# Six of sixteen projection tiles as pairs, with operand sums stored by the attention blocks and the mLSTM packed into the first six tiles

## The chip, the cores and the metric

The kernel runs on one core of one Trainium2 chip. The metric is the device time of one execution in microseconds (us), and lower is better. Engines are called by the names of the profile: PE is the matrix engine (PEld its weight loads), DVE the vector engine, ACT the scalar engine, POOL the general engine and SP the queue that issues most transfers.

## The reference

One inference step of a hybrid decoder layer on 512 prompt tokens and 8 x 4 sample tokens. In the kernel a token's column index runs over T = 544. An input projection feeds an mLSTM branch (4 heads of 512) and a sliding-window attention branch (32 heads of 64, window 128). Each branch is projected with a 2048 x 2048 matrix, gated, added, projected once more and normalised. The part that the change touches:

```python
br_m = hn.reshape(B, T, M_WIDTH) * jax.nn.sigmoid(o_m) * jax.nn.silu(z_m)
br_a = h_a * jax.nn.silu(z_a)
y = (jax.nn.sigmoid(g_m) * jnp.einsum('btc,cd->btd', br_m, w_proj_m)
     + jax.nn.sigmoid(g_a) * jnp.einsum('btc,cd->btd', br_a, w_proj_a))
out = jnp.einsum('btc,cd->btd', y, w_out)
return _layernorm(DN_ALPHA * x + out, ln_w, ln_b).astype(x.dtype)
```

Everything is float32. The kernel keeps that precision on PE by splitting each operand into a high and a low part (`hilo` for activations, `split` for weights: a cast on ACT and a subtraction on DVE) and adding three products: high x high, high x low, low x high.

## The kernel before

Activations lie transposed, channels on partitions and tokens along the row. A projection makes 128 output channels at a time, a column tile `ct`. There are two ways to do it.

**Plain** (`gemm`, `products`): 16 row blocks k of 128, three products each, two column halves of 272 tokens (HT = 272), so 96 matmuls into two PSUM banks. Weights come as two halves of 512 KB into three buffers (`wr`) and are split.

**Pairs** (`paired`, `prepare`, `half_product`, `gather`): two column tiles at once by a seven-product scheme of the Strassen kind over the 2 x 2 blocks (k below and above 8, tokens below and above 272). Each product is 8 row blocks x 3 = 24 matmuls. It needs sums of the operand's blocks, here called s1, n2, n3 and s4, each split into two parts, and sums of weight blocks, made by DVE (L665) and by accumulating transfers on POOL's queue (L663). The first input projection runs as pairs for most of the kernel; w_proj_m and w_out run four plain tiles first, while `operand_sums` builds their sums, and then pairs.

Helper work is written as generators. `spawn` puts one on a list, and `tick` advances each of the list by one step, from inside `products` (after every `every` row blocks) or after each product of `paired`. `drain` ticks until the list is empty. The order on each engine comes from a list scheduler that goes by the order of the program, by `high_priority` and by its own cost model. `issue_after(x)` makes the instructions of the block on x's engine stand behind x.

The stages, in order: the input projection in pairs, with the attention blocks beside it (`attention`, k = 0 to 15, each ending with a product on POOL, L848, and a store of its branch rows to d_bra, L849, on SP), then `sample_attention` and the sample heads of the mLSTM; w_proj_a with 16 plain tiles (from 1757 us), beside which `mlstm` runs the four prompt heads; w_proj_m; w_out and the layer norm. Nothing of w_proj_a runs as pairs, since the sums of its operand do not exist.

One head of the mLSTM: `values` (four transposes, split into vh, vl), `keys` (transposes, weighting L1427, split, 24 matmuls L1438 for the new state), `cells` (scores L1470, weighting L1473, split, matmuls L1483, `layernorm_rows`, transposes and row products L1494, store to d_brm). vh, vl, dm, ph and pl have one buffer each. The projection takes two of the four banks of pool psA per tile (`bank`), the helpers take banks of psB (`sm`, four). When the mLSTM has ended, `branch(d_brm, ...)` loads and splits the mLSTM branch for w_proj_m (L1377, then L245 and L246).

## Time and profile before

| | |
|---|---|
| time, median of 3 runs | 2464.07 us (2462.01 to 2466.16) |
| profiled execution, its own time | 2464.16 us |
| its span, first to last instruction | 2462.4 us |
| PE busy | 2433.8 us, 99% |
| DVE / ACT / POOL busy | 1884.0 / 1215.4 / 509.9 us |
| mean granted PE clock | 0.997 |
| transfers | 464.72 MB, mean 189 GB/s |

The profile is one execution recorded by the hardware. Busy time is the share in which an engine had an instruction at work; matmuls overlap, so a busy PE says that it was never idle, not that it ran at its peak. In a group of instructions, "xN" is their number, then come the total busy time, the mean length of one in ns, and the idle time of the engine ahead of them with what ended it. In a window's row the columns are the stretch, its length, the busy time and count of PE, PEld, DVE, ACT and POOL, the granted clock, the DMA share and GB/s. A line such as "SPq L187 <- DVE wl L201: 54.1, 10, 10.1" says who waited for whom: in total, how often, and the longest.

### The profile page before, as it was taken

How to read it: one execution, taken by the hardware profiler on the slowest of the kernel's cores; microseconds unless marked ns; L12 is line 12 of the kernel's file. 1: busy time of each engine (PE TensorE's matmuls, PEld its weight loads, DVE VectorE, ACT ScalarE, POOL GpSimd, SP SyncE). 2: the span in 40 equal slices, each digit the busy share in tenths (PEclk: the TensorE clock that was granted, in tenths of full speed). 3: DMA queues.
4: the chain of work that ended last, by engine and by line, in shares of the span. 5: the costliest groups of instructions: out<-in, count | busy, mean ns of one | idle time of the engine just before them, and what ended most of it. 6: DMA issues, size and time to landing. Idle time of an engine off the chain costs nothing.

```text
span 2462.4 us, 48812 instructions
## 1 busy us (share of the span) xinstructions
PE 2433.8 (99%) x19446; PEld 2378.9 (97%) x19446; DVE 1884.0 (77%) x2813; ACT 1215.4 (49%) x1994; POOL 509.9 (21%) x478
## 2 busy tenths in 40 slices
PE   8999999999999999999999999999999999999997
PEld 8999999999999999999999999999999999999996
DVE  7768888888888887787887888878855654767657
ACT  5456676676676564433433444544633333344431
POOL 3114334334333331211121122210000000110111
PEclk9999999999999999999999999999999999999998
DMA  6866666666666644578587687576755546888876
GB/s 177 201 173 158 163 161 144 162 161 150 160 154 160 155 124 138 143 217 247 179 242 244 163 241 229 176 251 217 246 171 173 187 147 210 226 218 253 220 221 188
DMA packets 557436, 464.72 MB, mean 189 GB/s; under 512 B 45592, under 2 KB 454344, under 8 KB 556952
## 3 DMA queue, kind: packets, MB, share of 16 engines
q1 hardware_dynamic: 540312, 402.09, 55.1%
q0 software_dynamic: 15696, 57.15, 12.1%
q8 instruction: 153, 2.51, 0.4%
q10 hardware_dynamic: 1200, 2.36, 0.3%
q14 instruction: 75, 0.61, 0.1%
HBM read 319.06 MB, written 96.31 MB: 169 GB/s over the span
## 4 chain that ended last, share of the span: by engine, by line
PE 94%; DMA 3%; DVE 2%; issue 1%; ACT 1%; SPq 0%; DVEq 0%; POOL 0%; ACTq 0%; POOLq 0%
PE bank L685 46%; PE bank L687 23%; PE bank L210 11%; PE sm L1438 2%; PE sm L210 1%; PE bank L1250 1%; PE sm L1470 1%; PE sm L795 1%; PE sm L1483 1%; PE sm L841 1%; DMA tx<-d_y 1%; DMA ty<-d_y 1%; DMA raw<-in_w_in 1%; PE sm L1800 1%; PE sm L821 1%
## 5 line engine op out<-in xcount | busy, mean ns | idle before, releaser
L200 ACT CAST wh<-raw 128x1024 fp32r<-128x1024 f32 x632 | 662.7, 1049 | 836.2 <-PE bank L685 686.6
L201 DVE TENSOR_TENSOR wl<-raw,wh 128x1024 fp32r<-128x1024 f32 x632 | 792.2, 1255 | 194.6 <-ACT wh L200 175.3
L685 PE MATMUL bank<-xk,wh 128*128 128x272 f32 x2336 | 322.7, 289 | 0.0
L665 DVE TENSOR_TENSOR raw<-raw,raw 128x1024 f32<-128x1024 f32 x238 | 304.1, 1279 | 12.6 <-DMA raw<-in_w_in 8.3
L685 PEld LDWEIGHTS bank<-xk,wh 128*128 128x128 f32 x2336 | 303.0, 188 | 2.8 <-issue 2.4
L704 POOL TENSOR_TENSOR ev<-p,ev 128x272 f32<-128x272 f32 x82 | 117.9, 1438 | 458.3 <-ACT ev L703 401.2
L685 PE MATMUL bank<-n2h,wh 128*128 128x272 f32 x656 | 169.8, 291 | 0.2 <-ACT wh L200 0.2
L687 PE MATMUL bank<-xk,wl 128*128 128x272 f32 x1168 | 169.7, 288 | 0.0
L685 PE MATMUL bank<-n3h,wh 128*128 128x272 f32 x656 | 169.6, 291 | 0.0
L685 PE MATMUL bank<-s1h,wh 128*128 128x272 f32 x656 | 169.1, 291 | 0.0
L685 PE MATMUL bank<-n2l,wh 128*128 128x272 f32 x656 | 167.7, 288 | 0.0
L685 PE MATMUL bank<-n3l,wh 128*128 128x272 f32 x656 | 167.6, 288 | 0.0
L685 PE MATMUL bank<-s1l,wh 128*128 128x272 f32 x656 | 167.3, 287 | 0.0
L685 PE MATMUL bank<-s4h,wh 128*128 128x272 f32 x656 | 167.2, 289 | 0.0
L685 PE MATMUL bank<-s4l,wh 128*128 128x272 f32 x656 | 167.0, 287 | 0.0
L687 PEld LDWEIGHTS bank<-xk,wl 128*128 128x128 f32 x1168 | 155.6, 188 | 0.1
L685 PE MATMUL bank<-a11h,wh 128*128 128x272 f32 x584 | 150.6, 290 | 0.0
L685 PE MATMUL bank<-a11l,wh 128*128 128x272 f32 x584 | 149.4, 288 | 0.0
L210 PE MATMUL bank<-bh,wl 128*128 128x272 f32 x704 | 147.5, 290 | 0.7 <-DVE wl L201 0.7
L210 PE MATMUL bank<-bh,wh 128*128 128x272 f32 x704 | 148.1, 289 | 0.0
L210 PE MATMUL bank<-bl,wh 128*128 128x272 f32 x704 | 148.0, 289 | 0.0
L663 POOL DMA_DIRECT2D raw<-raw x90 | 78.1, 868 | 291.8 <-DVE ev L712 202.2
(493 smaller groups left out, 5670.4 us busy)
## 6 DMA issues: line engine op xcount, KB each, us to landing
raw<-in_w_in SPq DMA_DIRECT2D x296, 512.0 KB
raw<-raw POOLq DMA_DIRECT2D x90, 512.0 KB, 4.8
C<-in_state_mlstm_C SPq DMA_DIRECT2D x32, 1024.0 KB
out<-C SPq DMA_DIRECT2D x64, 512.0 KB
raw<-in_w_proj_a SPq DMA_DIRECT2D x32, 512.0 KB
raw<-in_w_proj_m SPq DMA_DIRECT2D x32, 512.0 KB
raw<-in_w_out SPq DMA_DIRECT2D x32, 512.0 KB
d_v<-ev SPq DMA_DIRECT2D x16, 272.0 KB
```

The costliest lines, as they stand in the source:

```text
L200: state["cast"] = A.copy(wh[:, k:k + n], raw[:, k:k + n])
L201: state["split"] = V.tensor_tensor(out=wl[:, k:k + n], in0=raw[:, k:k + n], in1=r32(wh[:, k:k + n]), op=ALU.subtract)
L210: PE.matmul(ps[f][:, :w], a[:, kk], b(k, c, w), start=(k == 0 and n == 0), stop=(k == 15 and n == 2))
L663: G.dma_start(out=w[out][:], in_=w[b][:], accum_op=ALU.add)
L665: V.tensor_tensor(out=w[out][:], in0=w[a][:], in1=w[b][:], op=ALU.add)
L685: PE.matmul(ps, wh[:, k], x(p, k), start=(first and k == 0 and p == 0), stop=False, skip_group_check=True)
L687: state["end"] = PE.matmul(ps, wl[:, k], x(0, k), start=False, stop=(k == 7), skip_group_check=True)
L704: G.tensor_tensor(out=c22, in0=p1, in1=c11, op=ALU.subtract)
L795: PE.matmul(pp[:, c0 + w0:c0 + 256], qs[a][:, j * 128:j * 128 + 128], kx[:, k0:k0 + 256 - w0], start=(n == 0), stop=(n == 1))
L821: PE.transpose(pt[:, b * 128:b * 128 + 128], s_[:, b, 128:256], ident)
L841: PE.matmul(po[:, b * 128:b * 128 + n], VA[:, b], p_[:, 2 * b:2 * b + n // 128], start=(b == 0 and m == 0), stop=(b == 3 and m == 1), skip ...
L1438: PE.matmul(pp[:, 0:258], a[:, b * 128:b * 128 + 128], b_[:, b, f], start=(b == 0 and n == 0), stop=(b == 3 and n == 2))
```

## The change

- PSUM pools are closed and opened again: 4 + 4 banks up to the projection, six for helpers and two for the projection in it (`psum_pools(6)`), 4 + 4 again from the first pair. PSUM tiles of a new pool wait tile by tile for those that they replace.
- Attention blocks k = 8 to 15 load the first 240 columns of both halves of block k - 8's rows into a score buffer, form the four sums with DVE and store them to a new array, d_sa. `sample_attention` does the same for the 32 remaining columns ("rim" and samples), with one more load and four stores, all in pieces of 32 columns.
- w_proj_a: tiles 0 to 5 are plain with more frequent ticks (every row block in the first half, every second in the second). From tile 2 on PE's instructions of a tile stand behind the last mLSTM matmul that was written when the tile before began. Then `drain`; tiles 6 and 7 plain, while `stored_sums` loads and splits the 16 stored sums into the buffers that the mLSTM left; tiles 8 to 13 as three pairs; tiles 14 and 15 plain, with the loads and splits of the mLSTM branch beside them.
- mLSTM: the loads of values, keys and gate rows of a head are issued during the head before; the row output is a task of its own; queries are split beside the keys; two copies (L1442, L1519) go from DVE to ACT.

```diff
@@ -80,6 +80,7 @@
         kw = {"space": space} if space is not None else {}
         if space is None:
             kw["side"] = side or "right"
+        if space is not bass.MemoryType.DRAM:
             kw["reuse_waits"] = "tile"
         return stack.enter_context(tc.tile_pool(name=name, bufs=bufs, **kw))
...
-    psB = pool(es, "psB", 4, PSUM)
-    psA = pool(es, "psA", 4, PSUM)
-
     dr = pool(es, "dr", 1, bass.MemoryType.DRAM)
+
+    esPS = ExitStack()
+    es.callback(esPS.close)
+
+    def psum_pools(n):
+        return pool(esPS, nm("psB"), n, PSUM), pool(esPS, nm("psA"), 8 - n, PSUM)
 
...
+
+    psB, psA = psum_pools(4)
 
     def sm():
         return psB.tile([128, 512], F32, tag="sm", name=nm("sm"))
...
+    d_sa = dr.tile([8, 128, 4, T // 2], F32, name="d_sa")
...
-            products(ps, half, wh, wl, xh, xl, cols, every)
+            products(ps, half, wh, wl, xh, xl, cols, every[half] if isinstance(every, tuple) else every)
...
-    def paired(work, plain=None):
+    def paired(work, plain=None, rest=()):
 
         steps = [(w, n) for w in work for n in range(7)]
         ready = 0
...
+            if at == 4:
+                for _ in rest:
+                    pass
             half_product(w, n)
             with tc.high_priority(offset=AHEAD):
                 gather(w, n)
...
+        if k > 7:
+            sc = scores_tile()
+            nc.sync.dma_start(sc[:, 0:4:2, 0:PC], d_bra[k - 8].rearrange("p (c x) -> p c x", c=2)[:, :, 0:PC])
         for a in range(2):
...
         G.tensor_tensor(out=hT[:], in0=sz[:, 0:SEQ], in1=hT[:], op=ALU.mult)
         nc.sync.dma_start(d_bra[k][:, 0:SEQ], hT[:])
+        if k > 7:
+            spawn(branch_sums(sc[:, :, 0:PC], hT[:, 0:PC], hT[:, HT:SEQ], d_sa[k - 8][:, :, 0:PC]))
+
+    PC = SEQ - HT
+
+    def branch_sums(t_, r12, r22, to):
+        r11, s1, r21, s4 = (t_[:, j] for j in range(4))
+        V.tensor_tensor(out=s1, in0=r22, in1=r21, op=ALU.subtract)
+        V.scalar_tensor_tensor(r21, r11, -1.0, r21, op0=ALU.mult, op1=ALU.subtract)
+        V.tensor_tensor(out=r11, in0=r11, in1=s1, op=ALU.subtract)
+        V.tensor_tensor(out=s4, in0=r12, in1=r11, op=ALU.subtract)
+        if to is None:
+            for j in range(4):
+                nc.sync.dma_start(d_sa[:, :, j, PC:HT].rearrange("k p t -> p k t"), t_[:, j])
+        else:
+            nc.sync.dma_start(to, t_)
+        yield
...
+        left = kb[:].rearrange("p b x -> p (b x)")
+        rim = left[:, 1024:1536].rearrange("p (k t) -> p k t", k=16)
+        with tc.issue_after(state["load"].ins):
+            nc.sync.dma_start(rim, d_bra[:, :, PC:HT].rearrange("k p t -> p k t"))
         PTs = weightsT(0)
         before = iter(())
...
         nc.sync.dma_start(d_bra[:, :, SEQ:T].rearrange("k p t -> p k t"), gas[:])
+        t_ = left[:, 0:1024].rearrange("p (j k t) -> p j k t", j=4, k=8)
+        V.tensor_copy(t_[:, 0], rim[:, 0:8])
+        V.tensor_copy(t_[:, 2], gas[:, 0:8])
+        for _ in branch_sums(t_, rim[:, 8:16], gas[:, 8:16], None):
+            pass
...
-    _, bah, bal, g_ = branch(d_bra, act, lambda k: ev(), ahead)
+    (bah_, bal_), bah, bal, g_ = branch(d_bra, act, lambda k: ev(), ahead)
...
+    esPS.close()
+    psB, psA = psum_pools(6)
...
-                    PE.matmul(pp[:, 0:258], a[:, b * 128:b * 128 + 128], b_[:, b, f],
+                    state["cells"] = PE.matmul(pp[:, 0:258], a[:, b * 128:b * 128 + 128], b_[:, b, f],
...
-        V.tensor_copy(co[:, 256:512], p1[:, 0:256])
+        A.copy(co[:, 256:512], p1[:, 0:256])
...
-    def cells(h, kh, kl, qh, ql):
+    def cells(h, kh, kl, qh, ql, pre):
...
-                        PE.matmul(pp[:, 0:n], x_[c][:, b * 128:b * 128 + 128], y_[c][:, b * 128:SEQ],
+                        state["cells"] = PE.matmul(pp[:, 0:n], x_[c][:, b * 128:b * 128 + 128], y_[c][:, b * 128:SEQ],
...
             yield
+        if h + 1 < MH:
+            pre["v"] = load4(d_v, h + 1)
+        gt = load4(d_g, h)
...
-                            PE.matmul(pp[:, 0:258], x_[:, off:off + 128], y_[:, b, f],
+                            state["cells"] = PE.matmul(pp[:, 0:258], x_[:, off:off + 128], y_[:, b, f],
...
-            yield
-        gt = load4(d_g, h)
+            if js[-1] == 3 and h + 1 < MH:
+                pre["k"] = load4(d_k, h + 1)
+            yield
+        spawn(rows_out(h, hns, gt))
+
+    def rows_out(h, hns, gt):
         for c in range(4):
...
     def mlstm():
+        pre = {"v": load4(d_v, 0)}
+        for _ in range(2):
+            yield
+        pre["k"] = load4(d_k, 0)
+        yield
         for h in range(MH):
-            vts = load4(d_v, h)
+            vts, kts = pre["v"], pre["k"]
             spawn(decays(h))
-            yield
-            kts = load4(d_k, h)
             for c in range(4):
                 yield from values(h, c, vts[c])
             qts = load4(d_q, h)
             kh, kl, qh, ql = [], [], [], []
+
+            def two_parts(src, to):
+                a, b_ = t5(F32R), t5(F32R)
+                hilo(src[:], a[:], b_[:])
+                for tiles, t_ in zip(to, (a, b_)):
+                    tiles.append(t_)
+
             g_ = None
             for c in range(4):
-                a, b_ = t5(F32R), t5(F32R)
-                V.tensor_copy(a[:], kts[c][:])
-                V.tensor_tensor(out=b_[:], in0=kts[c][:], in1=r32(a[:]), op=ALU.subtract)
-                kh.append(a)
-                kl.append(b_)
+                two_parts(kts[c], (kh, kl))
                 n_ = keys(h, c, kts[c])
                 next(n_)
+                if c > 1:
...
+            for c in (2, 3):
+                two_parts(qts[c], (qh, ql))
             for _ in g_:
                 pass
             yield
-            yield from cells(h, kh, kl, qh, ql)
+            yield from cells(h, kh, kl, qh, ql, pre)
...
     wm, wa_, wo = kview("w_proj_m"), kview("w_proj_a"), kview("w_out")
     spawn(mlstm())
-    bmh = None
-    for ct in range(16):
-        sg = c5t()
-        nc.sync.dma_start(sg[:], d_sga[ct])
-        ps = gemm(wa_, ct * 128, bah, bal, every=2)
-        for p_, s_ in halves(ps, sg):
-            V.tensor_tensor(out=s_, in0=p_, in1=s_, op=ALU.mult)
-        nc.sync.dma_start(d_t[ct], sg[:])
-        if bmh is None and (not live or ct == 15):
-            drain()
-            esA.close()
-            es3, esE = ExitStack(), ExitStack()
-            act3 = pool(es3, "act3", 8)
-            bm_, bmh, bml, g_ = branch(d_brm, act3, lambda k: c5t() if k % 2 else ev())
-            spawn(g_)
-            c6 = pool(esE, "c6", 2)
-            esR = ExitStack()
-            wr2, pe_ = pool(esR, "wr2b", 3), pool(esR, "peb", 1)
-            tx = pool(esR, "txb", 2)
-    drain()
     def operand_sums(src, to, p):
 
...
@@ -1598,11 +1632,93 @@
     def operands(tiles, sums):
 
         low = [t[2:] for t in tiles]
-        return [side_by_side(tiles, 0), quarter(sums["s1"]), quarter(sums["n2"]), side_by_side(low, 0),
-                quarter(sums["n3"]), quarter(sums["s4"]), side_by_side(low, HT)]
+        s1, n2, n3, s4 = (x if callable(x) else quarter(x) for x in (sums[n] for n in ("s1", "n2", "n3", "s4")))
+        return [side_by_side(tiles, 0), s1, n2, side_by_side(low, 0), n3, s4, side_by_side(low, HT)]
+
+    def stored_sums(src, to, p):
+        f, e = ([[p.tile([128, 4, 2, HT], F32R, tag="act", name=nm("sum" + n)) for _ in range(2)] for n in "hl"]
+                for _ in range(2))
+        to["n2"], to["s1"], to["n3"], to["s4"] = (
+            (lambda q, k, t=t, j=j: t[q][k // 4][:, k % 4, j]) for t in (e, f) for j in range(2))
+
+        def load(n):
+            t_ = tx.tile([128, T], F32, tag="tx", name=nm("tx")) if n % 7 < 4 else ev()
+            G.dma_start(out=two(t_[:]), in_=src[n % 8][:, 0:2] if n < 8 else src[n % 8][:, 2:4])
+            return t_
+
+        ahead = [load(n) for n in range(7)]
+        for n in range(16):
+            for _ in range(2 if 8 <= n < 12 else 1):
+                yield
+            k, t_ = n % 8, ahead.pop(0)
+            hilo(two(t_[:]), *(t[k // 4][:, k % 4] for t in (e if n < 8 else f)))
+            if n + 7 < 16:
+                ahead.append(load(n + 7))
 
     def c6t():
         return c6.tile([128, T], F32, tag="c6", name=nm("c6"))
+
+    def plain_a(ct, **kw):
+        sg = c5t()
+        with tc.issue_after(state["load"].ins):
+            nc.sync.dma_start(sg[:], d_sga[ct])
+        ps = gemm(wa_, ct * 128, bah, bal, **kw)
+        for p_, s_ in halves(ps, sg):
+            V.tensor_tensor(out=s_, in0=p_, in1=s_, op=ALU.mult)
+        nc.sync.dma_start(d_t[ct], sg[:])
+
+    def pair_a(ct):
+
+        sgs = []
+
+        def early():
+            for c in (ct, ct + 1):
+                sg = c5t()
+                with tc.issue_after(state["load"].ins):
+                    nc.sync.dma_start(sg[:], d_sga[c])
+                sgs.append(sg)
+
+        def end(o1, o2):
+            for c, sg, o in zip((ct, ct + 1), sgs, (o1, o2)):
+                V.tensor_tensor(out=sg[:], in0=o[:], in1=sg[:], op=ALU.mult)
+                nc.sync.dma_start(d_t[c], sg[:])
+        return dict(wv=wa_, x=XA, cA=ct * 128, cB=ct * 128 + 128, scale=1.0, acc=True, end=end, early=early)
+
+    LEAD_A, PAIR_A, TAIL_A = 6, 8, 14
+    marks = []
+    for ct in range(LEAD_A):
+        marks.append(state.get("cells"))
+        with tc.issue_after(marks[ct - 1].ins) if ct > 1 and marks[ct - 1] else ExitStack():
+            plain_a(ct, every=(1, 2))
+    drain()
+    esA.close()
+    es3, esE = ExitStack(), ExitStack()
+    act3 = pool(es3, "act3", 8)
+    c6 = pool(esE, "c6", 2)
+    esR = ExitStack()
+    wr2, pe_ = pool(esR, "wr2b", 3), pool(esR, "peb", 1)
+    esB2 = ExitStack()
+    tx = pool(esB2, "txb", 4)
+    SA = {}
+    sums_ = stored_sums(d_sa, SA, act3)
+    next(sums_)
+    spawn(sums_)
+    for ct in range(LEAD_A, PAIR_A):
+        with tc.issue_after(state["cells"].ins):
+            plain_a(ct, every=2, prio=AHEAD)
+    esPS.close()
+    psB, psA = psum_pools(4)
+    XA = operands((bah_, bal_), SA)
+    paired([pair_a(ct) for ct in range(PAIR_A, TAIL_A, 2)], state["split"], rest=sums_)
+    state["end"] = None
+    drain()
+    esB2.close()
+    tx = pool(esR, "txc", 2)
+    bm_, bmh, bml, g_ = branch(d_brm, act3, lambda k: ev() if k % 5 < 3 else c6t())
+    spawn(g_)
+    for ct in range(TAIL_A, 16):
+        plain_a(ct, every=2, prio=AHEAD)
+    drain()
 
     def merged(ct, plain=False):
 
```

More of the change, by code (lines that the diff above doesn't have):

```diff
@@ L1515, in mlstm @@
             kh, kl, qh, ql = [], [], [], []
+            def two_parts(src, to):
[3 more added lines that the diff above has]
+                    tiles.append(t_)
             g_ = None
             for c in range(4):
-                a, b_ = t5(F32R), t5(F32R)
-                V.tensor_copy(a[:], kts[c][:])
-                V.tensor_tensor(out=b_[:], in0=kts[c][:], in1=r32(a[:]), op=ALU.subtract)
-                kh.append(a)
-                kl.append(b_)
+                two_parts(kts[c], (kh, kl))
                 n_ = keys(h, c, kts[c])
                 next(n_)
+                if c > 1:
+                    two_parts(qts[c - 2], (qh, ql))
                 if g_ is not None:
@@ L1529, in mlstm @@
                 yield
-            for c in range(4):
-                a, b_ = t5(F32R), t5(F32R)
-                hilo(qts[c][:], a[:], b_[:])
-                qh.append(a)
-                ql.append(b_)
+            for c in (2, 3):
+                two_parts(qts[c], (qh, ql))
             for _ in g_:
```

## The prediction

> **What bounds the kernel now.** I read the page first (shares, chain), then the waits of the matmul engine, then busy time by stretch, then groups of instructions inside the projection stage.
>
> ```profile
> span 2462.4 us, 48812 instructions
> ...
> PE 2433.8 (99%) x19446; PEld 2378.9 (97%) x19446; DVE 1884.0 (77%) x2813; ACT 1215.4 (49%) x1994; POOL 509.9 (21%) x478
> ...
> PE 94%; DMA 3%; DVE 2%; issue 1%; ACT 1%; SPq 0%; DVEq 0%; POOL 0%; ACTq 0%; POOLq 0%
> ```
>
> ```profile
> PE bank L210 <- DVE wl L201: 0.7, 1, 0.7
> ```
>
> ```profile
> 520.00:920.00 400.00, 400.00 (x3221) 400.00 (x3220) 337.44 (x486) 260.32 (x475) 146.53 (x110) 1.00 0.64 153
> 850.00:900.00 50.00, 50.00 (x405) 50.00 (x404) 44.00 (x61) 32.03 (x59) 18.17 (x13) 1.00 0.59 146
> 950.00:1000.00 50.00, 50.00 (x369) 46.00 (x368) 38.43 (x63) 25.46 (x51) 7.04 (x4) 1.00 0.34 96
> 1757.00:2013.00 256.00, 255.30 (x2032) 252.93 (x2032) 160.10 (x400) 99.39 (x191) 10.62 (x20) 1.00 0.53 175
> 2125.00:2215.00 90.00, 90.00 (x721) 90.00 (x721) 62.81 (x81) 36.09 (x44) 12.60 (x12) 1.00 0.83 213
> 2200.00:2250.00 50.00, 50.00 (x402) 50.00 (x401) 34.16 (x47) 21.73 (x29) 3.91 (x4) 1.00 0.94 268
> ```
>
> PE carries the chain (94%). From 1752 to 2110 us it waited once, 0.7 us (the second fence). The windows give the stretch, then PE, weight loads, DVE, ACT, POOL (count), granted clock, DMA share, GB/s. The three stages that the edit touches have PE without a gap: the attention blocks (520 to 920; DVE 84%), the mLSTM beside the projection's tiles (1757 to 2013), and pairs (2125 to 2215). So time changes in two ways only: fewer matmuls, or a PE gap that is not there now.
>
> **Part 1, three pairs for six tiles.** A plain tile is 16 row blocks x 3 products x 2 column halves = 96 matmuls of 272 columns, so two tiles are 192. A pair is 7 products x 24 = 168. Three pairs drop 72 matmuls. In the pair window 721 take 90.00 us, 124.8 ns each: 72 x 0.1248 = 9.0 us less.
>
> [...]
>
> Everything else adds no matmul. The question is what of the 9.0 us the rest gives back.
>
> **Part 2, the mLSTM in six tiles.** First the work.
>
> ```profile
> L210 PE MATMUL bank<-bl,wh 128*128 128x272 f32 x340 | 73.0, 291 | 0.0
> L210 PE MATMUL bank<-bh,wh 128*128 128x272 f32 x340 | 72.9, 290 | 0.0
> L210 PE MATMUL bank<-bh,wl 128*128 128x272 f32 x338 | 71.8, 291 | 0.7 <-DVE wl L201 0.7
> ```
>
> ```profile
> L201 DVE TENSOR_TENSOR wl<-raw,wh 128x1024 fp32r<-128x1024 f32 x34 | 41.5, 1219 | 18.8 <-ACT wh L200 18.7
> L1066 DVE BATCH_NORM_STATS2 lnst<-sm 128x6 f32<-128x256 f32 x32 | 13.2, 425 | 0.0
> L1560 DVE TENSOR_TENSOR c<-bank,c 128x272 f32<-128x272 f32 x32 | 12.6, 430 | 12.4 <-PE bank L210 12.2
> ...
> L1494 DVE TENSOR_TENSOR t<-sm,t 128x512 f32<-128x512 f32 x16 | 10.2, 683 | 16.5 <-PE sm L1493 16.5
> ...
> L1442 DVE COPY f<-sm 128x256 f32<-128x256 f32 x16 | 6.8, 422 | 24.1 <-PE sm L1438 24.1
> L1519 DVE CAST t<-t 128x512 fp32r<-128x512 f32 x16 | 6.7, 420 | 1.5 <-DMA t<-d_k 1.5
> ...
> L1068 DVE SCALAR_TENSOR_TENSOR lns<-lns 128x1 f32<-128x1 f32 x16 | 3.5, 219 | 0.5
> ```
>
> Between 1757 and 2013 the projection has 340 + 340 + 338 = 1018 matmuls, 127 us at 124.8 ns (10.6 tiles); the other 129 us are the mLSTM's. Six tiles are 576 matmuls, 71.9 us, so the packed stage is 129 + 72 = 201 us of PE. DVE there has 160.1 now. It loses 4.6 tiles: 9.2 splits x 1.22 = 11.2 and 9.2 evacuations x 0.43 = 4.0. It also loses the copies of L1442 and L1519 that go to ACT, 6.8 + 6.7. That leaves 131 us, 65% of 201. ACT has 99.4 now; with some 16 us added for them it is at 57% even if it lost nothing. Neither engine is the bound by its sum. The head's program takes 15 steps (four values, four keys, one more, three scores, three cells), so 3 + 60 + 4 for the last rows, some 69 with the ends. Six tiles give 6 x (8 + 4) = 72 steps, so it fits.
>
> Order is the danger: a head change, where PE now lives on projection matmuls.
>
> ```profile
> 1883.65 4.00 PE bank L210 x32
> 1888.75 4.50 PE bank L210 x36
> 1895.18 2.88 PE bank L210 x23
> 1899.75 4.98 PE bank L210 x40
> 1906.90 2.68 PE sm L1438 x22
> ```
>
> ```profile
> 1893.96 0.69 DVE L1451 TENSOR_TENSOR f<-sm,cc 128x512 f32<-128x512 f32 x1 [1.55 <-PE sm L1449]
> ...
> 1907.65 2.07 DVE L246 TENSOR_TENSOR t<-t,t 128x512 fp32r<-128x512 f32 x3
> ```
>
> These are pieces of the chain and of DVE's timeline. From the end of one head's cells to the next head's first key product (1906.90) PE does 16.4 us of projection in the four pieces, while DVE runs almost gapless from 1893.96 to 1907.65. After the edit six steps lie there, on average 6 x 1.0 = 6.0 us of projection, and some 42 transposes at 0.124 (400.00 / 3221 in the first window above), 5.2 us: 11.2 us of cover. DVE must do one row normalisation (two statistics of 0.43, eight small operations of at most 0.22, about 2.3), four value splits and four row products at 0.68, the decay's sum (0.69), three operations of 0.68 on the first key, a weight split (1.22) and two evacuations (0.79): 12.5 us. Short by 1.3, with about 2 us of hand-overs 3.3, for each of three changes: at worst 9.9 us. Against it: matmuls of the same tile may be taken early (6 us on average are left of a tile), the row products are now a task behind the next head's first step, and value and key loads are issued during the cells before. The mark on the cells two tiles back only stops the projection from running out too soon. I take a seventh, +1.4 us, nearer to zero because today's waits are zero at nearly the same DVE share (160.1 of 256, 63%); bounds 0 and +9.9.
>
> **Part 3, two banks instead of four for the projection.** A tile must now be evacuated before the next begins.
>
> ```profile
> 2065.72 0.79 DVE L1560 TENSOR_TENSOR c<-bank,c 128x272 f32<-128x272 f32 x2 [3.79 <-PE bank L210]
> 2066.68 1.23 DVE L201 TENSOR_TENSOR wl<-raw,wh 128x1024 fp32r<-128x1024 f32 x1 [0.17 <-ACT wh L200]
> ```
>
> I read the first from the timeline (its pair takes 0.79, one 0.43). Bare, PE waits about 0.43 plus a hand-over of 0.1; behind a weight split, 1.2 more. There are seven such boundaries, tile 0/1 to 6/7. Five lie inside the mLSTM, whose own matmuls fill them; 5/6 and 6/7 are bare, 0.55 each. I take +1.1 us; bounds 0.5 and 7 x 2.0 = 14 us.
>
> [...]
>
> **Part 4, sums in the attention blocks.** Blocks 8 to 15 add one load, four DVE operations and one store each; the sample rows get copies, sums, one load and four stores.
>
> ```profile
> L1587 DVE TENSOR_TENSOR tx<-tx 128x272 f32<-128x272 f32 x2 | 0.9, 430 | 0.0
> ```
>
> ```profile
> SPq L187 <- DMA raw<-raw: 112.3, 22, 11.2
> SPq L849 <- POOL hT L848: 74.5, 9, 10.8
> ```
>
> Four sums of 240 columns cost at most 4 x 0.43 = 1.7 us, eight blocks 13.8 us on DVE, which goes from 84 to 88% there. The window from 850, with 44.00 of 50, already keeps PE at 50.00, and splits are prepared three products (9 us) ahead: zero. SP gets the new store behind the branch store (L849), which already holds that queue for up to 10.8 us; weight loads (L187) stand behind it. The sums add about 2 us to such a hold. The load waits for a score buffer, released some steps before. The cover is the six buffered weight halves; if it goes, 8 x 2 = 16 us is the far bound. I take 0. The sample columns move in pieces of 128 B, but DMA is 0.34 busy from 950 to 1000: 0, at most +2.
>
> **Part 5, the tail's two hand-overs.** The stored sums (16 loads of 272 KB on POOL's queue, 16 splits of 0.72 on DVE) must be ready between 27 and 36 us after tile 6 begins. The mLSTM branch's 16 loads and splits, formerly spread from 1836 on, now fit between the last pair and the end of the first tile of the next product, some 36 us.
>
> ```profile
> L1377 SPq DMA_DIRECT2D ev<-d_brm x8: 319/320/891, 1836.1 to 2024.4; - x8
> ```
>
> ```profile
> L246 DVE TENSOR_TENSOR bl<-c,bh x8: 716/724/726, 2026.9 to 2056.2; 128x544 fp32r<-128x544 f32 x8
> ```
>
> Each is 16 x 0.72 = 11.6 us of DVE in 36. Bytes: 4.4 MB, about 3 MB of weights and 1 MB of other traffic in 36 us, 233 GB/s; 2200 to 2250 carried 268 GB/s with PE at 50.00. I take 0; bounds 0 and +4, one late transfer each.
>
> **Sum.** -9.0 + 1.4 + 1.1 = -6.5 us. The profiled execution took 2464.16 us (span 2462.4 and 1.8 around it), 0.1 above the median of 2464.07: 2457.6 us, 0.26% less. About 0.2%, 4.9 us, can be told from no change, so the stalls may reach 4.1 us before the gain is lost to view.
>
> **Rivals.**
>
> (a) Starved head changes: the cover of part 2 fails and 5 to 9.9 us come back. For: DVE's gapless stretch above. Against: DVE's 65% and the loose tile. With 7.5 + 1.1: 2463.7, within 0.2%.
>
> (b) Two banks bubble, the slower end. At each of the seven boundaries the evacuation stands behind a split or an mLSTM operation on DVE and PE has nothing else: 2.0 us each, 14 us. With part 2's 1.4, -9.0 + 14.0 + 1.4 = +6.4: 2470.5. It decides for slower than before from 7.6 / 7 = 1.1 us a boundary, and visibly from 1.8. Against: 129 us of mLSTM matmuls stand beside 72 us of projection.
>
> (c) SP's queue in the attention blocks: the added holds starve weights for 1.5 us in each of the eight blocks: +12, so -6.5 + 12 = +5.5, 2469.6. Against: PE waits nowhere there though holds reach 10.8 us.
>
> (d) The work of parts 4 and 5 costs nothing and the stalls do not appear: 2455.1.
>
> **Numbers.** Forecast 0.42, (d) 0.12, (a) 0.22, (b) 0.14, (c) 0.10. Faster by over 0.2%: (d), and four fifths of the forecast and a little of (a), 0.48. Within 0.2%: the rest of the forecast and most of (a), 0.28. Slower: (b), (c): 0.24. The faster case's own range is 2454 to 2460. For 8 in 10 the range runs from 2454 (below (d)) to 2470: it takes in (a) and (c) and leaves out about half of (b) and what lies past the bounds.
>
> **What would show it.** PE with 72 fewer matmuls; the stage from the first plain tile to the first pair about 225 us (129 + 8 x 12); PE waits inside it below 3 us, on evacuations at 5/6 and 6/7; PE at 50.00 of 50 in 520 to 920; the projection's last six tiles as pairs at 21 us each. I am wrong if PE's waits on DVE or ACT in that stage sum to over 5 us, if L187's waits on SP reach PE, or if the next product's first tile waits for its operand.

## The result

The changed kernel takes 2472.66 us (median of 7 runs, 2470.57 to 2474.05) against 2464.07 for the kernel before (7 runs, 2461.53 to 2466.16): a ratio of 1.0035, 95% interval 1.0023 to 1.0047, 8.6 us slower. The forecast was 2457.6, the range 2454 to 2470. The sign was wrong, and the time lies past the upper end. The profiled execution took 2474.05 us (span 2472.3), the longest of the seven.

The page of the changed kernel, span, busy times and shares of the chain:

```profile
span 2472.3 us, 48919 instructions
...
PE 2430.4 (98%) x19374; PEld 2372.8 (96%) x19374; DVE 1911.0 (77%) x2856; ACT 1245.6 (50%) x2060; POOL 524.2 (21%) x503
...
PE 88%; DMA 5%; DVE 3%; issue 2%; ACT 1%; SPq 1%; POOL 0%; DVEq 0%; POOLq 0%; ACTq 0%
```

The 72 matmuls are gone (19446 to 19374), yet PE's busy time fell by only 3.4 us while the span grew by 9.9. PE's share of the chain fell from 94 to 88%, and DMA's rose from 3 to 5. New waits ate more than the saved matmuls. The waits of PE over the whole execution of the changed kernel (in total, times, longest):

```profile
PE bank L692 <- ACT wh L207: 5.9, 4, 1.9
...
PE bank L692 <- DVE ev L717: 2.1, 1, 2.1
PE bank L217 <- DVE wl L208: 2.1, 2, 1.4
PE sm L1459 <- DMA t<-d_v: 1.7, 1, 1.7
PE sm L805 <- DVE mn L807: 1.5, 1, 1.5
PE bank L217 <- DVE c L1667: 0.9, 2, 0.5
```

Only the last stands in the prediction's sum. The windows of the changed kernel that answer to those shown before:

```profile
520.00:920.00 400.00, 395.45 (x3174) 394.36 (x3173) 336.05 (x510) 255.43 (x471) 138.56 (x107) 1.00 0.67 163
850.00:900.00 50.00, 50.00 (x405) 50.00 (x404) 41.92 (x65) 31.96 (x59) 17.44 (x14) 1.00 0.62 155
950.00:1000.00 50.00, 49.37 (x449) 46.00 (x448) 38.39 (x62) 25.95 (x52) 6.79 (x5) 1.00 0.38 102
1768.00:2024.00 256.00, 252.38 (x1999) 249.05 (x1999) 169.00 (x395) 123.88 (x245) 21.97 (x35) 1.00 0.62 197
2125.00:2215.00 90.00, 90.00 (x722) 90.00 (x721) 61.94 (x83) 36.15 (x45) 12.50 (x12) 1.00 0.84 214
2200.00:2250.00 50.00, 50.00 (x402) 50.00 (x401) 31.14 (x42) 18.62 (x23) 6.11 (x6) 1.00 0.87 243
```

The attention blocks had 400.00 of 400 and now have 395.45. An average DVE share (336.05 of 400, as low as before) does not show why. First starts of the same work in the two traces tell how the delay grows:

| first start, us | before | after | difference |
|---|---|---|---|
| last attention block's store to d_bra | 911.7 | 918.2 | +6.5 |
| sample attention's gate load | 914.4 | 928.2 | +13.8 |
| attention branch's loads for w_proj_a | 1739.2 | 1750.3 | +11.1 |
| first plain tile of w_proj_a | 1757.1 | 1768.2 | +11.1 |
| first store of y (w_proj_m) | 2094.6 | 2105.7 | +11.1 |
| first product of w_out | 2254.9 | 2265.1 | +10.2 |

So there are two findings. Some 11 us are lost before the projection starts, in the stages that hold only the new sums. And in the stage where 72 matmuls were saved, almost nothing is gained. Of the signs that the prediction named, PE at 50.00 of 50 in 520 to 920 failed, and PE's waits between the first plain tile and the first pair came to 3.7 us instead of less than 3.

**Where the blocks lose: 700 to 750 us.** The next three fences are the SP queue by time: of before, of the changed kernel, and of the run e5 below, in which one load was moved. L769, L779 fetch the key rows of the next head group, L187 and L194 weights, L847 the rows for the sums.

```profile
706.62 1.09 SPq L769 DMA_DIRECT2D s<-d_ka  x2
...
710.62 4.33 SPq L187 DMA_DIRECT2D raw<-in_w_in  x2
```

```profile
706.81 0.54 SPq L847 DMA_DIRECT2D s<-d_bra  x1
710.82 4.39 SPq L194 DMA_DIRECT2D raw<-in_w_in  x2
...
716.01 2.44 SPq L779 DMA_DIRECT2D s<-d_ka  x2
```

```profile
706.08 1.12 SPq L779 DMA_DIRECT2D s<-d_ka  x2
...
710.10 4.37 SPq L194 DMA_DIRECT2D raw<-in_w_in  x2
```

In the changed kernel the sums' load takes the free score buffer at 706.81. The key load gets the next one, which DVE's last read of it (L841) sets free at 715.20:

```profile
714.66 0.54 DVE L841 TENSOR_TENSOR P<-s,P 128x384 fp32r<-128x384 f32 x1
```

A weight load that holds SP for 4.39 us stands ahead of it as well, and ends at the same moment. So it starts at 716.01 instead of 706.62; the buffer alone accounts for 8.6 of these 9.4 us. ACT and DVE pay. ACT by time (L252 casts the keys, L207 weights), and two of DVE's waits in 690 to 760 us, both of the changed kernel:

```profile
723.38 0.62 ACT L252 CAST k<-s 128x512 fp32r<-128x512 f32 x1 [7.16 <-DMA s<-d_ka]
723.91 1.04 ACT L207 CAST wh<-raw 128x1024 fp32r<-128x1024 f32 x1
```

```profile
DVE k L253 <- ACT k L252: 5.0, 1, 5.0
DVE s L807 <- DMA d_sa<-s: 3.8, 1, 3.8
```

ACT's cast of the keys waits 7.2 us for the load (1.0 in the same window of before). The weight cast behind it starts the moment it is done, with no wait of its own: it had only been standing in line, and so had the next pieces of weights that PE needs. DVE stands behind that cast for 5.0 us, and 3.8 us more for the sums' own store, which must leave its score buffer before scores can be written there. The windows of before and of the changed kernel at that place:

```profile
700.00:750.00 50.00, 50.00 (x405) 50.00 (x404) 42.65 (x61) 33.64 (x62) 17.21 (x14) 1.00 0.70 166
```

```profile
700.00:750.00 50.00, 45.45 (x357) 44.36 (x356) 37.43 (x60) 29.24 (x55) 15.12 (x12) 1.00 0.67 159
```

PE lost 4.55 us, and DVE and ACT were both less busy, not more: they waited.

**Where the tail loses: 2048 to 2064 us.** ACT by time in the changed kernel (L252 casts the mLSTM branch, L207 weights), then the chain of waits there:

```profile
2047.44 1.05 ACT L207 CAST wh<-raw 128x1024 fp32r<-128x1024 f32 x1 [0.35 <-PE bank L692]
2054.09 0.65 ACT L252 CAST bh<-ev 128x544 fp32r<-128x544 f32 x1 [5.59 <-DMA ev<-d_brm]
...
2055.18 1.04 ACT L207 CAST wh<-raw 128x1024 fp32r<-128x1024 f32 x1
```

```profile
2048.63 6.01 DMA c<-d_brm
...
2055.18 1.05 ACT wh L207
...
2056.28 2.74 PE bank L692 x16
2059.02 1.81 PE bank L694 x8
```

It is the same pattern: a cast for a product that starts only after two more plain tiles (24 us) waits 5.59 us for its transfer, and the last pair's weight cast stands behind it. PE waits 1.8 us.

### The profile page after: what moved, and what is told of

It reads as the page before. It is cut to its first block, busy times and chain, and to the rows that moved or that the text cites. A ratio compares the mean times of both kernels' runs of the same rounds, so it can differ in the third digit from the quotient of the medians.

```text
span 2472.3 us, 48919 instructions
## 1 busy us (share of the span) xinstructions
PE 2430.4 (98%) x19374; PEld 2372.8 (96%) x19374; DVE 1911.0 (77%) x2856; ACT 1245.6 (50%) x2060; POOL 524.2 (21%) x503
## 4 chain that ended last, share of the span: by engine, by line
PE 88%; DMA 5%; DVE 3%; issue 2%; ACT 1%; SPq 1%; POOL 0%; DVEq 0%; POOLq 0%; ACTq 0%
PE bank L692 44%; PE bank L694 22%; PE bank L217 8%; PE sm L1480 2%; PE sm L217 1%; PE sm L1512 1%; PE bank L1289 1%; PE sm L1528 1%; PE sm L805 1%; PE sm L854 1%; DVE wl L208 1%; PE sm L1916 1%; PE sm L831 1%; PE sm L1294 1%; DMA ty<-d_y 1%
## 5 line engine op out<-in xcount | busy, mean ns | idle before, releaser
L207 ACT CAST wh<-raw 128x1024 fp32r<-128x1024 f32 x641 | 671.8, 1048 | 833.7 <-PE bank L692 701.8
L672 DVE TENSOR_TENSOR raw<-raw,raw 128x1024 f32<-128x1024 f32 x244 | 311.9, 1279 | 17.5 <-DMA raw<-in_w_proj_a 4.7
L670 POOL DMA_DIRECT2D raw<-raw x96 | 83.1, 866 | 327.5 <-DVE ev L719 203.6
L692 PEld LDWEIGHTS bank<-n2h,wh 128*128 128x128 f32 x656 | 123.3, 188 | 3.8 <-ACT wh L207 3.1
L692 PEld LDWEIGHTS bank<-n3h,wh 128*128 128x128 f32 x656 | 123.4, 188 | 1.8 <-issue 1.4
L692 PEld LDWEIGHTS bank<-s4h,wh 128*128 128x128 f32 x656 | 123.2, 188 | 1.0 <-issue 1.0
```

The source lines that it names most:

```text
L207: state["cast"] = A.copy(wh[:, k:k + n], raw[:, k:k + n])
L670: G.dma_start(out=w[out][:], in_=w[b][:], accum_op=ALU.add)
L672: V.tensor_tensor(out=w[out][:], in0=w[a][:], in1=w[b][:], op=ALU.add)
L692: PE.matmul(ps, wh[:, k], x(p, k), start=(first and k == 0 and p == 0), stop=False, skip_group_check=True)
```

## Experiments

The theory before the runs was that the sums inside the attention blocks cost the time, with the packed projection innocent. The rivals were the packed projection itself, the rim's small transfers, and the hand-over.

**e1, the sums taken out.**

```diff
-        if k > 7:
-            sc = scores_tile()
-            nc.sync.dma_start(sc[:, 0:4:2, 0:PC], d_bra[k - 8]...)
...
-            spawn(branch_sums(...))
-                (and the rim's load, copies, sums and stores)
-            G.dma_start(out=two(t_[:]), in_=src[n % 8][:, 0:2] if n < 8 else src[n % 8][:, 2:4])
+            G.dma_start(out=two(t_[:]), in_=two(src[n]))      # src = d_bra
```

> The changed kernel without any sums in the attention blocks and the sample rows (no load, no DVE operation, no store there); the pairs of the projection take rows of d_bra of the same size instead of the stored sums, so its pairs multiply wrong numbers. Theory S (the sums cost the time, in the attention stage): the first plain tile of the projection is back at about 1757 us and the whole is 11 us under the changed kernel, about 2461.5 us, some 2.5 under the kernel before. Rival P (the packed projection costs it, two banks and the hand-overs): 2471 to 2473, with the first plain tile still late or the stage after it longer.

Measured: 2465.47 us, ratio 1.0002 (0.9993 to 1.0011), before 2464.92 on that chip. The sums cost about 8 us, and the projection as changed gives nothing back: +0.5, where the prediction's parts 1 to 3 had -6.5.

**e2, the sums alone.**

```diff
 (kernel before)
+    d_sa = dr.tile([8, 128, 4, T // 2], F32, name="d_sa")
+        (the blocks' load, sums and store; the rim's load, copies, sums and stores)
```

> The kernel before with the sums of the attention blocks and sample rows added (load, four DVE operations, store to d_sa) and nothing else; nobody reads d_sa. Theory S: 9 to 12 us slower than before, 2473 to 2476, with the matmul engine waiting on ACT and DVE near 700 to 750 us. Rival P: within 2 us of before, 2464 to 2466.

Measured: 2473.65 us, ratio 1.0038 (1.0025 to 1.0051): +8.7. e1 and e2 agree from both sides.

**e3, no rim.**

```diff
-        with tc.issue_after(state["load"].ins):
-            nc.sync.dma_start(rim, d_bra[:, :, PC:HT].rearrange("k p t -> p k t"))
...
-        V.tensor_copy(t_[:, 0], rim[:, 0:8])
-        V.tensor_copy(t_[:, 2], gas[:, 0:8])
-        for _ in branch_sums(t_, rim[:, 8:16], gas[:, 8:16], None):
-            pass
+        (in `old_rows`: four stores of constants to the rim of d_sa)
```

> The changed kernel without the sums of the rim and sample columns in the sample attention (its load, two copies, four sums and four stores); the rim of d_sa is filled from constants by four stores early in the attention stage, so the pairs are wrong in 32 of 272 columns. From the end of the last block's store (918 us) to the first plain tile (1768 us) the changed kernel loses 4.6 us against before. If the rim's work does it: about 2468. If the late start of the sample attention does it (its tiles lie where the last block's score buffer is, which the store to d_sa holds): 2471 to 2473.

Measured: 2472.53 us, ratio 1.0031 (1.002 to 1.0042), +7.6 against +8.6 for the changed kernel. The rim is worth about 1 us at most, and the ranges of the two kernels overlap.

**e4, the mLSTM branch's casts behind the weight casts.**

```diff
-                hilo(st[:], hs[k // 4][:, k % 4], los[k // 4][:, k % 4])
+                with tc.issue_after(behind().ins) if behind else ExitStack():
+                    hilo(st[:], hs[k // 4][:, k % 4], los[k // 4][:, k % 4])
...
-    bm_, bmh, bml, g_ = branch(d_brm, act3, lambda k: ev() if k % 5 < 3 else c6t())
+    bm_, bmh, bml, g_ = branch(d_brm, act3, lambda k: ..., behind=lambda: state["cast"])
```

> The changed kernel with one order edge: the casts of the mLSTM branch on ACT stand behind the newest weight cast written so far, so not ahead of the last pair's weight casts. If ACT's queue was blocked there by a cast that waits for its load (6.0 us at 2048), the gap of 1.9 us in 2050 to 2060 goes and with it the slow matmuls that follow: 3 to 3.5 us, about 2469.3. If the transfers are the limit of that hand-over, the wait only moves to the first tile of the next product: 2472 to 2473.

Measured: 2472.27 us, ratio 1.0035 (1.0022 to 1.0047). The gap after the pairs is gone in its trace; 2050 to 2100 us, first the changed kernel, then e4:

```profile
2050.00:2100.00 50.00, 48.15 (x374) 47.93 (x373) 29.89 (x49) 22.84 (x37) 1.50 (x2) 0.97 0.89 277
```

```profile
2050.00:2100.00 50.00, 50.00 (x403) 50.00 (x402) 33.71 (x59) 25.24 (x42) 2.22 (x3) 1.00 0.90 274
```

The median moved by only 0.4 us, less than the runs scatter. The profiled execution, the shortest of six (2471.01), lost time to a lower clock at two other places, where the changed kernel's stayed at 1.00 (last section). e7 and e9 test the same edit again.

**e5, the next keys loaded first.** In block 11 the next group's key and value loads take the score buffer ahead of the sums' load.

```diff
+        if k == 11:
+            state["kv"] = kv_load(3)
         if k > 7:
             sc = scores_tile()
...
-        (loads at the start of kv_head)
+        kraw, vraw = state.pop("kv", None) or kv_load(kvh)
```

> The changed kernel with one reordering: in block 11 the next head group's key and value rows are loaded into a score buffer ahead of the sums' load. Theory B (the sums' extra score buffer pushes that load onto the other buffer, free 8 us later; ACT's key cast waits at the head of its queue with the weight casts behind it): the 7.2 us wait of ACT at 717 us and most of the 4.5 us gap of the matmul engine in 700 to 750 go, the last block ends at about 912 us instead of 918, and the whole is 5 to 6.5 us shorter, about 2467. Rival H (the buffer is held by the store to d_sa, which the next block's scores wait for): no change, 2472 to 2474.

Measured: 2468.46 us, before 2465.39 on that chip: +3.1 instead of +8.6. The ratio's interval is wide, 1.0029 (1.0001 to 1.0057), because one of ten runs took 2500.39, at a mean granted clock of 0.926. The window of e5 shows the stage whole again:

```profile
700.00:750.00 50.00, 50.00 (x405) 50.00 (x404) 44.24 (x66) 33.43 (x62) 17.09 (x14) 1.00 0.75 181
```

DVE does the same sums in it, 44.24 us busy against 42.65 in before, and PE loses nothing. Before and behind this window, from 150 to 900 us, PE is busy without a gap as well. So the four sums are free for PE there, as the prediction had it; the order of two loads was not. This settles the larger part of the cost.

**e6, the store does not hold the score buffer.** The block's store to d_sa is read from a tile that is not a score buffer (so the stored values are not the sums).

```diff
-            nc.sync.dma_start(to, t_)
+            for j in (0, 2):
+                nc.sync.dma_start(to[:, j:j + 2], hold[:, 0:480].rearrange("p (c x) -> p c x", c=2))
```

> The changed kernel with the block's store to d_sa read from the branch tile instead of the sums, in two transfers of the same bytes, so the score buffer is free as soon as the DVE sums end; the stored sums are wrong. Rival H: DVE's wait for the store (3.8 us at 740) goes and so does most of the gap: 2467 to 2469. It also frees the sample attention's tiles earlier: 1 to 2 us more. Theory B: the key load is where it was, the gap at 717 stays and only 1 to 2 us go: 2471 to 2472.

Measured: 2470.21 us, ratio 1.0016 (1.0007 to 1.0025), +4.8, between the two ranges expected. The hold is real but the lesser part: PE has 47.24 of 50 in 700 to 750 us. e5 and e6 remove pieces of one chain of waits, so their gains need not add.

**e7, e1 with the edge of e4.**

```diff
 (e1)
+    (the edge of e4)
```

> The kernel without sums (of the first experiment, 2465.5) with the order edge of the fourth (branch casts behind weight casts). If the hand-over after the last pair gives back some 3 us of the pairs' 9: 2462 to 2463, the three pairs in 63 to 64 us. If it is limited by transfers: 2465 to 2466.

Measured: 2462.13 us, ratio 0.999 (0.998 to 0.9999): -3.3, against +0.5 for e1: 3.8 us by the medians. The traces show less. The two profiled executions differ by 1.6 us. PE's waits at the hand-over in e1, 1.8 us, are gone in e7, but 1.1 us of waiting comes up in the next product, and the clock fell once in e1, at another place. So the size of the hand-over is not settled by this pair. This run is also the projection part without the sums and without the hand-over. From 1.2 us ahead of its first plain tile (1758.4) to its first pair, and the three pairs:

```profile
1757.20:1987.90 230.70, 226.71 (x1795) 223.40 (x1794) 148.77 (x369) 113.78 (x233) 18.37 (x31) 1.00 0.61 197
1987.90:2051.00 63.10, 63.10 (x505) 63.10 (x505) 43.15 (x55) 26.93 (x33) 9.30 (x9) 1.00 0.78 196
```

**e8, e1 with four banks for each instead of six and two.**

```diff
-    psB, psA = psum_pools(6)
+    psB, psA = psum_pools(4)
```

> The kernel without sums with four and four PSUM banks in the packed stage instead of six and two. If two banks for the projection cost a gap at every tile boundary (rival of the prediction): 4 to 8 us shorter, 2458 to 2461. If they cost only the two bare boundaries, 0.5 to 0.6 us each, as the trace shows: 1 us shorter at best, 2464.5; and if the helpers need the six banks: 2 us or more longer, 2467 and up.

Measured: 2472.32 us, ratio 1.0032 (1.0019 to 1.0045): 6.4 us worse than e1. PE's largest wait in 1750 to 2080 us of e8:

```profile
PE sm L1513 <- ACT t L1100: 5.4, 2, 2.7
```

By this line the row normalisation (ACT, L1100) is what the next cells wait for with four banks. The 0.9 us of waits on the evacuations at the two bare boundaries are gone, but the helpers lose more. The run changes both shares at once, so it says what two banks are worth to the helpers against the projection, and not what each would do alone.

**e9, e5's order and e4's edge together.** The whole computation.

```diff
 (changed kernel)
+    (the edit of e5)
+    (the edge of e4)
```

> Whole computation. The changed kernel with two of the edits tried alone so far: the next key and value rows are loaded ahead of the sums' load in block 11, and the mLSTM branch's casts stand behind the last pair's weight casts. If the two costs are separate and add (4.2 us from the first, 0.4 to 3.3 us from the second), the time is 2466 to 2469, still above the kernel before, and the rest is lost at the start of the sample attention and of the projection. If the hand-over's 0.4 us was the true size, 2468 to 2469; if the 3.3 us seen without the sums was, 2465 to 2466.

Measured: 2464.68 us, ratio 1.0 (0.9991 to 1.0009). Two edits of order take the 8.6 us away, and the kernel stands level with the one before, below each range that was expected. By the medians the edge is worth 3.8 us here (+3.1 in e5, -0.7 now), 3.8 in e7 against e1, and 0.4 in e4. The traces don't support 3.8: in the profiled execution of e5, without the edge, PE waits only 0.5 us at the hand-over, and the first product of w_out starts at 2257.0 us against 2256.4 in e9. The 5.2 us between these two executions arise later, where e5 has a wait of 2.5 us on DVE at 2303 and a fall of the clock behind it. So that the two edits together bring the kernel level is measured; how much of it is the edge stays open.

**e10, the last row's sums formed late.** Block 15 makes no sums; they are formed from the branch rows 7 and 15 where the stored sums are split.

```diff
 (e9)
-        if k > 7:
+        if 7 < k < 15:
...
+            if n == 15:
+                V.tensor_tensor(out=r22, in0=r22, in1=r21, op=ALU.subtract)
+                (and the other three sums, in place, and their four splits)
```

> Whole computation. As the run before it in this call, and block 15 makes no sums: row 7 of the stored sums is formed from the branch rows 7 and 15 where the stored sums are split, beside tiles 6 and 7. Theory (the late start of the sample attention after block 15 is what is left of the sums' cost): the sample attention's gate load is issued about 10 us earlier, and 2 to 4 us go, 2462 to 2465, no slower than the kernel before. Rival (the loss between 900 and 1100 us is the rim's loads, sums and stores): less than 1 us goes.

Measured: 2467.18 us, ratio 1.0009 (1.0 to 1.0018), 2.5 us above e9 with ranges that overlap, and above the 2462 to 2465 expected. The sample attention's gate load, of before, the changed kernel and e10:

```profile
L932 SPq DMA_DIRECT2D gas<-d_bra x1: 376/376/376, 914.4 to 914.4; - x1
```

```profile
L962 SPq DMA_DIRECT2D gas<-d_bra x1: 376/376/376, 928.2 to 928.2; - x1
```

```profile
L969 SPq DMA_DIRECT2D gas<-d_bra x1: 376/376/376, 912.8 to 912.8; - x1
```

The late start is gone, so the sums of block 15 made it, and the first plain tile comes 2.2 us earlier than in e9 (1759.3 against 1761.6). But DVE's added sums and splits stand in front of the first pair's weight split, for which PE waits 1.5 us: 47.60 of 50 in 1950 to 2000 us against 49.09 in e9. The mechanism was as the theory said, and part of what it returned was given back there. But the profiled execution is the shortest of e10's eleven (2464.05) and 0.9 us below that of e9, so its trace does not hold the 2.5 us. The eleven times go with their mean granted clock: 2464.05 and 2465.66 at 0.998, 2471.72 and 2472.89 at 0.995. The time did not get better by the medians; why is not shown.

**e11, the first values two ticks later.**

```diff
 (e10)
         pre = {"v": load4(d_v, 0)}
-        for _ in range(2):
+        for _ in range(4):
             yield
```

> Whole computation. As the run before it, and the first head's value transposes stand two ticks later in the first projection tile, of the three that the 72 ticks leave over. Theory (transposes placed ahead of tile 0's matmuls wait for the first values' load, 2.0 us): 1.5 to 2 us less than the run before, 2460 to 2463. Rival (the ticks run out and the last rows come after tile 5): PE idles between tiles 5 and 6 and the time is the same or up to 3 us longer.

Measured: 2473.61 us, ratio 1.0035 (1.0022 to 1.0047), 6.4 us worse than e10, past the rival's 3. Its profiled execution is the longest of five (2477.88). The window of e11 in which the first pair should run:

```profile
2000.00:2050.00 50.00, 45.93 (x355) 45.44 (x354) 32.28 (x41) 17.87 (x21) 7.17 (x7) 0.97 0.77 200
```

The loads of rows 7 and 15 for the stored sums move from 1966.5 to 1977.3 us, since they go into what the mLSTM leaves, and the first pair comes to wait, 3.7 us on a weight split: PE loses 4 us between 2000 and 2050. The clock falls behind this wait and at two other places before 2400 us. The three ticks that the count of steps left over are no real slack, because what follows the mLSTM starts later by each. The wait for the first values only fell from 2.0 to 1.2 us.

## Why the prediction was wrong

**Part 1, the pairs: right.** 63.10 us for three pairs (e7), 21.0 each, as foretold, and 72 fewer matmuls. In the changed kernel itself the stage up to the first pair and the three pairs with the hand-over took:

```profile
1768.20:1997.26 229.06, 225.44 (x1785) 222.11 (x1784) 147.75 (x367) 112.52 (x231) 18.37 (x31) 1.00 0.60 197
1997.26:2064.00 66.74, 64.89 (x506) 64.67 (x505) 46.32 (x59) 29.68 (x38) 8.97 (x9) 0.97 0.80 206
```

**Part 3, two banks: right, and the slower rival (b) with it refuted.** The chain of the changed kernel at the boundaries 5/6 and 6/7:

```profile
1971.77 0.45 DVE c L1667
...
1972.27 12.15 PE bank L217 x95
...
1984.44 0.45 DVE c L1667
...
1985.03 12.23 PE bank L217 x96
```

0.5 and 0.6 us at the bare boundaries (0.55 each were predicted). The rival had 2.0 at each of seven. And e8, which gives the projection four banks and the helpers four, is 6.4 us slower than e1.

**Part 2, the packing: a size off, at another place.** From first plain tile to first pair 229.5 us (e7, 1758.4 to 1987.9) against 225 + 1.1: +3.4 (229.1 and +3.0 in the changed kernel), inside the bounds 0 to 9.9, not the 1.4 taken. Rival (a) put it at the head changes; the 2 us of hand-overs in the 3.3 for each were an estimate that no run shows. PE's waits in 1740 to 2080 us of e7 show them free:

```profile
PE sm L1445 <- DMA t<-d_v: 2.0, 1, 2.0
PE bank L216 <- DVE c L1653: 0.9, 2, 0.5
PE bank L216 <- DVE wl L207: 0.7, 1, 0.7
PE sm L1514 <- ACT t L1100: 0.3, 1, 0.3
```

The largest is at the very start. The first head's values are loaded in the stretch where the branch's 16 loads run, and PE's transposes, placed among tile 0's matmuls, wait for them.

**Part 5, the hand-overs: taken as 0 with +4 as the far bound; 3.6 in the changed kernel's trace.** Other traces show less at that place (1.8 us of waits in e1, 0.5 in e5). It was argued by amounts (11.6 us of splits in 36, 233 GB/s), and the amounts were no obstacle: e4 moves 274 GB/s from 2050 to 2100 with PE at 50.00. What failed is the order on ACT: work with at least 24 us to spare stood ahead of work that was due at once.

**Part 4, the sums: taken as 0; 8.7 by e2, 8 by e1.** This is the step that turned the sign. The prediction priced DVE's work (free, e5 shows it) and SP's holds in front of weight loads (rival (c), 1.5 us in each of eight blocks). Rival (c) had the right stage and a size of the right order (12 us) but not the mechanism; that its 2469.6 comes near the measured time is luck. In the runs the loss is at one block out of eight, where a new head group begins, and it came through the buffer. The prediction says "The load waits for a score buffer, released some steps before" and goes on to the weight loads behind SP's holds. It did not ask which load is pushed behind it, nor what stands behind the cast that waits for that load. About 4.5 us are lost there (45.45 of 50). Most of the rest is lost behind the blocks: against before, PE is busy 1.3 us less in 900 to 950 and 2.6 us less in 950 to 1100. There the sample attention's loads stand on SP behind the last block's sums, their store (924.16) and a weight load that waits for DVE, so the gate load goes out at 928.2 instead of 914.4; without sums in block 15 (e10) it goes out at 912.8.

**Sum.** -9.0 + 1.1 + 3.4 + 3.6 + 8.7 = +7.8, against +8.6 measured; 3.6 is the hand-over as its trace shows it (1.8 of waiting, 1.8 of slow matmuls, below). The terms come from medians and from single executions, so the sum is a rough one. The sizes of the rim and of the sample attention's late start are not settled one by one: e3 gives about 1 us for the first, and in e10's trace the second returned 2.2 us up to the first plain tile, of which 0.9 was left at the end.

## What to carry to other kernels

When a new transfer takes a buffer from a small rotating pool, ask which older transfer now gets the next buffer and when that one comes free, what holds the queue in front of it, and which instructions stand behind the one that waits for it on the same engine (on ACT a weight cast stood behind a key cast that waited 7.2 us); the new arithmetic itself cost PE nothing here. Work that is due late must be placed behind work that is due soon on the engine that casts for both, even where there is ample time for both. Two such edits of order were worth the whole loss (e9), and no average of a stage would have shown them.

## What the runs showed of the hardware

A short wait cost twice. After PE's wait of 1.8 us at the hand-over, the granted clock of the changed kernel fell:

```profile
2056.00:2058.00 2.00, 1.72 (x13) 1.72 (x14) 1.87 (x4) 1.88 (x4) 0.00 (x0) 0.95 1.20 300
2058.00:2060.00 2.00, 2.00 (x11) 2.00 (x11) 1.86 (x3) 1.14 (x3) 0.00 (x0) 0.50 0.58 213
2060.00:2062.00 2.00, 2.00 (x13) 2.00 (x13) 1.63 (x3) 1.23 (x2) 0.00 (x0) 0.69 0.53 153
```

Forty matmuls took 6.79 us (2056.28 to 2063.07) where they take 5.0 elsewhere, so the 1.8 us became 3.6. The clock stood at 0.50 from about 1.5 us after work had resumed (2057.75 against 2056.28), behind a wait of 1.85 us. In e1 a gap of the same kind, 1.4 us, left the clock at 1.00.

The other traces show the same event. Between 30 and 2400 us the clock falls once in e1, e2, e3, e5 and e6, twice in e4 and e8, three times in e11, and never in before, e7, e9 and e10. Each time it falls to 0.50 right behind a wait of PE, and each time some 1.7 us are lost by it (the shortfall of the clock, summed over stretches of 5 us). The waits ahead of it were 1.85 us (the changed kernel) to 3.7 us (e11). But a wait of that length did not always bring it. The wait for the first head's values was 2.0 us in e1, e4 and e7: the clock fell behind it in e1 (0.66 in 1765 to 1770) and in e4 (0.84 and 0.82 in 1770 to 1780), and stayed at 1.00 in e7. In e4 it fell behind a wait of 2.3 us as well (0.87 and 0.79 in 930 to 940), where the changed kernel's wait of 2.1 us left it at 1.00. So e4's profiled execution lost 3.4 us in this way and the changed kernel's 1.7. That is one reason why a gain of 2 us can be lost among executions; what decides whether the clock falls, no run here shows.
